# Fixed places in the engines' order for the transposes, the rounded stationary and gate times up of an expert block

## The chip, the cores and the metric

One core of a Trainium2 chip runs the whole program in one launch. The metric is the time of an execution on the device in microseconds; where several were measured, their median. The engines are named as in the profile: PE is TensorE's matmul row, PEld its weight loads, DVE is VectorE, ACT is ScalarE, POOL is GpSimd, SP is SyncE, which issues the weight transfers.

## What is computed

Two float32 model blocks, one behind the other, on 256 tokens of width 1024. The first has two layers of feed-forward, four mixers and feed-forward. The second has a pooling mixer with a feed-forward, and a delta-rule mixer with a mixture of experts. The change lies in the last of these alone:

```python
N_EXPERTS, TOP_K, EXPERT_FF = 8, 2, 3584
logits = (t @ router_w) + router_b
top_vals, top_idx = lax.top_k(logits, TOP_K)
gates = jnp.sum(one_hot(top_idx, N_EXPERTS) * softmax(top_vals)[..., None], axis=1)
for e in range(N_EXPERTS):
    y = (silu(t @ w_gate[e]) * (t @ w_up[e])) @ w_down[e]
    out = out + gates[:, e:e + 1] * y
```

## The kernel before, in words

The first 1.6 ms hold the other layers and don't change. In the expert stage (function `short`) the eight experts are taken in the order of their token counts. For each, the tokens that chose it are gathered into the columns of a stationary tile `XG`. An expert's 3584 inner columns are done in seven blocks of 512, so there are 56 steps. Each step streams 12 weight tiles of 128x1024 float32 (512 KB each) from HBM into a ring of 23 buffers `raw` (8 + 11 + 4): four for the gate product, four for the up product, four for the down product.

Products are made in a rounded float32 format. So each weight tile is split in `halves` (lines 328 to 338): ScalarE writes the rounded tile `hi` (line 336), VectorE writes the rest `lo = raw - hi` (line 337), and only then can `raw` be loaded again. There are five `hi` and four `lo` buffers. Tokens are split likewise. Experts of which `FEW` is true (six of eight) have at most 64 tokens: their rounded tokens and the rests lie side by side in one 128-column stationary, so a `hi` or `lo` tile is multiplied once, and the two halves of the result are added by a matmul with a constant matrix `BOTH`. The last of the eight tiles of gate and up is used unsplit, as full float32 against `XF` (two matmul rows for each 512 columns). So a few-token step has 11 `hi` and 11 `lo`. The two other experts split tokens in two stationaries and make three products for each tile, 12 `hi` and 12 `lo`.

One step's way: `gate_up` (line 1931) fills two PSUM banks `gu`; `finish` (line 1957) makes `sl`, first Silu of the gate bank on ScalarE (line 1959), then gate times up, times the row scale, on VectorE (line 1960). `down` (line 1964) turns `sl` by four TensorE transposes into the PSUM tile `x`, splits that into the stationary `hh` (`split`, lines 362 and 363: the rounded part on ScalarE, the rest on VectorE, in the same tile for few-token experts, in `hl` for the others), splits four weight tiles and multiplies them into two PSUM banks `y`. After the seventh block `scatter` adds `y` to the result `ACC`.

The steps are laid over each other: the loop at the end of `short` calls `gate_up` of a block first, then `down` of the block before; the new block's `finish` is called inside that `down`. A scheduler then sets each engine's order by its own estimates of time; each engine runs its list strictly in that order, so an instruction that waits holds all behind it. The helper `queued` (line 1917) adds an order without a wait: its instruction may not stand earlier on its engine than the one named. Before, two things are tied so: the copy of the gate bank for `BOTH` (line 1929), and the Silu, behind the `hi` of the down product's first tile.

Of the kernel before, what the change touches and what calls it, by code (L numbers as in the profile page):

```python
# [9 lines left out]
F32 = mybir.dt.float32  # L10
F32R = mybir.dt.float32r
I32 = mybir.dt.int32
BF16 = mybir.dt.bfloat16
AF = mybir.ActivationFunctionType
OP = mybir.AluOpType
# [3 lines left out]
P = 128  # L19
# [4 lines left out]
NE = 8  # L24
# [37 lines left out]
FEW = [r not in (1, 2) for r in PLACES]  # L62
# [186 lines left out]
class _K:  # L249
# [78 lines left out]
    def halves(self, raw, parts=1):  # L328

        nc = self.nc  # L330
        self.npart += 1
        hi, lo = [self.T(ps[self.npart % len(ps)], [P, 1024], n, F32R) for ps, n in ((self.his, "hi"), (self.los, "lo"))]
        n = 1024 // parts
        for i in range(parts):
            c = slice(i * n, i * n + n)
            self.last_hi = nc.scalar.activation(hi[:, c], raw[:, c], AF.Copy)  # L336
            nc.vector.tensor_tensor(lo[:, c], raw[:, c], hi[:, c].bitcast(F32), OP.subtract)  # L337
        return hi, lo

    def chunk(self, ap):  # L340
# [1501 lines left out]
    def short(self, HH, HL, ACC, RS, keyp, keyl, GTp, BOTH, where, st):  # L1842
# [3 lines left out]
        nc, tc = self.nc, self.tc  # L1846

        def open_(name, bufs):
            return st.enter_context(tc.tile_pool(name=name, bufs=bufs))

        pool, p1 = open_("few", 2), open_("few1", 1)
# [65 lines left out]
        def queued(ins, first):  # L1917

            if first is not None:
                self.tc.add_manual_dep(  # L1920
                    ins.ins, first.ins.name,
                    mybir.DependencyInfo(mybir.DependencyClass.NoSync, mybir.DependencyReason.DATA),
                    reason="order on an engine")

        both = []

        def copy_gate(ps):
            both.append(self.T(p1, [P, 512], "both"))
            queued(nc.scalar.activation(both[-1], ps, AF.Copy), self.last_hi)

        def gate_up(e, fb, XG, RX, XF):
            gu = []
            for m in range(2):
                ps = self.T(self.psg, [P, 512], "gu")
                for q in range(2):
                    raws = [self.load_half(where(e)[fb * 6 + m * 2 + q], j) for j in range(2)]
                    whole = m and q and FEW[e]
                    ch = [self.halves(r) for r in raws[0:1 if whole else 2]]
                    if m and not q and FEW[e]:
                        copy_gate(gu[0])  # L1940
                    for kk in range(4):
                        k = q * 4 + kk
                        c = slice((kk % 2) * 512, (kk % 2) * 512 + 512)
                        if whole and kk > 1:
                            self.mm(ps, ps, XF[:, kk - 2, :], raws[1][:, c], False, k == DT - 1)
                            continue
                        wh, wl = ch[kk // 2]
                        self.mm(ps, ps, XG[:, 0, k, :], wh[:, c], k == 0, False)
                        if not FEW[e]:
                            self.mm(ps, ps, XG[:, 1, k, :], wh[:, c], False, False)  # L1950
                        self.mm(ps, ps, XG[:, 0, k, :], wl[:, c], False, k == DT - 1)
                gu.append(ps)
            if FEW[e]:
                self.mm(gu[0], gu[0], BOTH, both[-1], True, True)
            sl = self.T(pool, [P, 512], "sl")

            def finish(hi):

                queued(nc.scalar.activation(sl, gu[0], AF.Silu, scale=RX), hi)
                nc.vector.scalar_tensor_tensor(sl, gu[1], RX, sl, OP.mult, OP.mult)  # L1960

            return sl, finish

        def down(e, fb, sl, ya, OT, fin=None):
            ps = self.T(self.psx, [P, 512], "x")
            p4 = ps.rearrange("p (a b) -> p a b", a=4)
            hh = self.T(pool, [P, 4, P], "hh", F32R)
            if FEW[e]:
                n = slice(0, 64)
                for i in range(4):  # L1970
                    self.mm(ps, p4[:, i, n], sl[:, i * P:i * P + P], BOTH[:, n], True, True)
                self.split(p4[:, :, n], hh[:, :, n], hh[:, :, 64:])
            else:
                for i in range(4):
                    self.tr(p4[:, i, :], sl[:, i * P:i * P + P])
                hl = self.T(p1, [P, 4, P], "hl", F32R)
                self.split(p4, hh, hl)
            end = (e, fb) == (NE - 1, 6)
            if end:
                raws = [self.load_half(where(e)[fb * 6 + 4 + j // 2], j % 2, 2) for j in range(4)]  # L1980
                self.gb, self.fin = self.raw(), self.raw()
                nc.sync.dma_start(self.gb, self.A["prow"][:, 24:24 + D].partition_broadcast(P))
            for n in range(2):
                if not end:
                    raws = [self.load_half(where(e)[fb * 6 + 4 + n], j) for j in range(2)]
                    ch = [self.halves(raws[0])]
                    if n == 0 and fin:
                        fin(self.last_hi)
                    ch.append(self.halves(raws[1]))
                for i in range(4):  # L1990
                    c = slice((i % 2) * 512, (i % 2) * 512 + 512)
                    first, last = fb == 0 and i == 0, fb == 6 and i == 3
                    if end and i % 2 == 0:
                        w = self.halves(raws[2 * n + i // 2], 2)
                    wh, wl = w if end else ch[i // 2]
                    self.mm(ya[n], ya[n], hh[:, i, :], wh[:, c], first, False)
                    if not FEW[e]:
                        self.mm(ya[n], ya[n], hl[:, i, :], wh[:, c], False, False)
                    self.mm(ya[n], ya[n], hh[:, i, :], wl[:, c], False, last)
            if fb == 6:  # L2000
                for n in range(2):
                    scatter(e, n, ya[n], OT, end)

        def scatter(e, n, y, OT, end):
            yh = self.T(late[0], [P, 512], f"yh{n}", F32R)
            yl = self.T(late[0], [P, 512], f"yl{n}", F32R)
            self.split(y, yh, yl)
            c = slice(n * 512, n * 512 + 512)
            for t in range(2):
                ps = self.T(self.psx, [P, 512], "x")  # L2010
                self.mm(ps, ps, OT[:, t, :], yh, True, False)
                self.mm(ps, ps, OT[:, t, :], yl, False, True)
                nc.vector.scalar_tensor_tensor(ACC[:, t, c], ps, GTp[:, t, e:e + 1], ACC[:, t, c], OP.mult, OP.add)
                if end:
                    self.squares(ACC, t, n)

        steps = [(e, fb) for e in range(NE) for fb in range(7)]
        G = []
        for _ in gather([0]):
            pass  # L2020
        ya, pend = None, None
        for e, fb in steps + [(None, None)]:
            if e is not None:
                if (e, fb) == (0, 5):
                    self.early.close()
                    early.close()
                    px.append(open_("fewx2", 1))
                    late.append(open_("fewy", 1))
                sl, fin = gate_up(e, fb, G[e][0], *G[e][2:4])
            if pend is None:  # L2030
                fin(None)
            else:
                pe, pf, psl, pg = pend
                if pf == 0:
                    ya = [self.T(self.psy, [P, 512], f"y{n}") for n in range(2)]
                down(pe, pf, psl, ya, pg, fin if e is not None else None)
                es = [1] if pe == 0 else [pe + 1, pe + 2] if pe % 2 and pe < NE - 1 else None
                if pf == 4 and es:
                    for _ in gather(es):
                        pass  # L2040
            pend = (e, fb, sl, G[e][1]) if e is not None else None

    def moe(self, HH, HL, ACC, RS, GT, key, ci, few):
        nc, tc = self.nc, self.tc
# [148 lines left out]
```

## Time and profile before

| | |
|---|---|
| time, median of 3 runs | 2562.23 us (2560.03 to 2562.67) |
| the profiled execution | 2560.89 us, of which the span 2559.0 us |
| instructions | 45163 |
| expert stage, from the first gate matmul | 1629.2 us to the end of the span |
| mean granted TensorE clock | 0.994 |

The span runs from the first to the last instruction; the rest of an execution's time lies around it. The views used below: the page's busy shares; stretches of the span, chosen here to begin and end at a Silu (`sl` on ScalarE), which happens once in a step; the list of who waited for whom; and the timeline of one engine, in which like instructions next to each other are merged into one row, with the idle time ahead of the row and what ended it in brackets.

### The profile page before, as it was taken

The page shows a single profiled execution, that of the slowest core. Times are in us where ns is not written, and L with a number is a line of the kernel's source. Part 1 is how long each engine was busy: PE and PEld are TensorE (multiplying, and loading weights), DVE is VectorE, ACT ScalarE, POOL GpSimd, SP SyncE. Part 2 cuts the span into 40 slices and gives each one's busy share as a digit, 9 for nine tenths or more (in the row PEclk, how much of TensorE's full clock was granted, in tenths as well). Part 3 has the DMA queues.
Part 4 walks back from the last instruction along what each step waited for, and adds up shares of the span by engine and source line. Part 5 has one row for each costly group of instructions (what it writes and reads, how often), then busy time and mean ns, then how long its engine had stood idle before and what let it go on. Part 6 is the DMA issues. An engine that isn't in the chain of part 4 may idle for free. (4 is left out here: it accounts for less than half of the span.)

```text
span 2559.0 us, 45163 instructions
## 1 busy us (share of the span) xinstructions
PE 2501.5 (98%) x16795; PEld 2200.1 (86%) x16795; DVE 1933.5 (76%) x2621; ACT 1554.7 (61%) x2218; POOL 94.9 (4%) x99
## 2 busy tenths in 40 slices
PE   8999999999999999999999999899999999999997
PEld 8999899999999799999999998777766876677764
DVE  7657566666666667666765786799988898889887
ACT  5445464444445365445544675788777777777776
POOL 0003000000002100000000010000000000000000
PEclk9999999999999999999999999899999999999999
DMA  7655124555665233555566434899999999999994
GB/s 237 191 182 164 66 91 131 184 185 184 185 188 166 83 97 113 189 184 184 169 187 188 144 122 167 310 404 409 408 392 377 360 342 402 388 384 356 366 381 169
DMA packets 166915, 603.13 MB, mean 236 GB/s; under 512 B 18736, under 2 KB 19264, under 8 KB 166688
## 3 DMA queue, kind: packets, MB, share of 16 engines
q1 hardware_dynamic: 165792, 596.92, 66.5%
q0 software_dynamic: 896, 3.27, 0.4%
q8 instruction: 133, 2.18, 0.4%
q14 instruction: 94, 0.77, 0.1%
HBM read 596.96 MB, written 2.10 MB: 234 GB/s over the span
## 5 line engine op out<-in xcount | busy, mean ns | idle before, releaser
L337 DVE TENSOR_TENSOR lo<-raw,hi 128x1024 fp32r<-128x1024 f32 x1086 | 1290.2, 1221 | 337.7 <-ACT hi L336 329.9
L336 ACT ACTIVATE hi<-raw 128x1024 fp32r<-128x1024 f32 x1086 | 1104.2, 1052 | 621.9 <-issue 324.8
L264 PE MATMUL m<-xh,hi 128*128 128x256 f32 x1760 | 495.7, 282 | 8.5 <-ACT xh L365 7.9
L264 PE MATMUL m<-xh,lo 128*128 128x256 f32 x1760 | 495.8, 282 | 2.6 <-DVE lo L337 2.5
L264 PE MATMUL m<-xl,hi 128*128 128x256 f32 x1760 | 495.3, 282 | 1.8 <-DVE xl L366 1.8
L264 PE MATMUL gu<-hi,XG 128*128 128x512 f32 x1036 | 373.4, 399 | 0.2
L264 PE MATMUL gu<-lo,XG 128*128 128x512 f32 x812 | 347.5, 430 | 5.9 <-DVE lo L337 5.3
L264 PEld LDWEIGHTS m<-xh,hi 128*128 128x128 f32 x1760 | 333.5, 189 | 9.2 <-ACT xh L365 8.3
L264 PEld LDWEIGHTS m<-xh,lo 128*128 128x128 f32 x1760 | 333.2, 189 | 3.5 <-DVE lo L337 3.5
L264 PEld LDWEIGHTS m<-xl,hi 128*128 128x128 f32 x1760 | 333.1, 189 | 2.4 <-DVE xl L366 2.4
L264 PE MATMUL mm<-hl,hi 128*128 128x256 f32 x880 | 248.2, 282 | 0.0
L264 PE MATMUL mm<-hh,lo 128*128 128x256 f32 x880 | 248.2, 282 | 0.0
L264 PE MATMUL mm<-hh,hi 128*128 128x256 f32 x880 | 247.6, 282 | 0.0
L264 PE MATMUL mm<-xh,hi 128*128 128x256 f32 x832 | 240.6, 290 | 6.0 <-DVE x L1133 3.1
L264 PE MATMUL mm<-xl,hi 128*128 128x256 f32 x832 | 239.3, 288 | 0.0
L264 PEld LDWEIGHTS gu<-hi,XG 128*128 128x128 f32 x1036 | 195.4, 189 | 50.2 <-ACT hi L336 7.8
L264 PE MATMUL mm<-xh,lo 128*128 128x256 f32 x832 | 237.9, 286 | 0.1
L264 PEld LDWEIGHTS gu<-lo,XG 128*128 128x128 f32 x812 | 153.1, 189 | 94.4 <-DVE lo L337 59.9
L264 PE MATMUL y<-hi,hh 128*128 128x512 f32 x448 | 193.4, 435 | 0.0
L264 PE MATMUL y<-lo,hh 128*128 128x512 f32 x448 | 181.3, 410 | 6.5 <-DVE lo L337 6.3
L264 PEld LDWEIGHTS mm<-hl,hi 128*128 128x128 f32 x880 | 168.2, 191 | 0.0
L264 PEld LDWEIGHTS mm<-hh,lo 128*128 128x128 f32 x880 | 168.2, 191 | 0.0
(589 smaller groups left out, 3501.6 us busy)
## 6 DMA issues: line engine op xcount, KB each, us to landing
raw<-in_moe SPq DMA_DIRECT2D x668, 512.0 KB, 6.4
raw<-in_ffn SPq DMA_DIRECT2D x330, 512.0 KB, 3.5
raw<-in_win SPq DMA_DIRECT2D x56, 512.0 KB, 3.5
raw<-in_dnin SPq DMA_DIRECT2D x32, 512.0 KB, 3.8
raw<-in_wout SPq DMA_DIRECT2D x16, 512.0 KB, 3.5
raw<-in_pin SPq DMA_DIRECT2D x8, 512.0 KB, 3.6
raw<-in_dnout SPq DMA_DIRECT2D x8, 512.0 KB, 3.6
raw<-in_moe SPq DMA_DIRECT2D x8, 256.0 KB, 6.2
```

What stands on the lines that cost most here:

```text
L264: ins = self.nc.tensor.matmul(out, lhsT=lhsT, rhs=rhs, start=start, stop=stop)
L336: self.last_hi = nc.scalar.activation(hi[:, c], raw[:, c], AF.Copy)
L337: nc.vector.tensor_tensor(lo[:, c], raw[:, c], hi[:, c].bitcast(F32), OP.subtract)
```

## The change

`halves` keeps the `lo` instruction as it kept the `hi`. In `gate_up` the first `hi` and `lo` of the gate product's second half are remembered (its third tile). `finish` becomes a function of its own with a place for each of its two instructions: the Silu stays behind the `hi` of the down product's first tile; gate times up is now tied behind the `lo` of the down product's last tile. In `down` the first transpose is tied behind the last `y` matmul of the block before; the rounded part and the rest of `hh` are tied behind the remembered `hi` and `lo` of the next block's gate product, save in the very last block. The helper `split` is written out for this. No instruction is added or removed.

```diff
@@ halves
-            nc.vector.tensor_tensor(lo[:, c], raw[:, c], hi[:, c].bitcast(F32), OP.subtract)
+            self.last_lo = nc.vector.tensor_tensor(lo[:, c], raw[:, c], hi[:, c].bitcast(F32), OP.subtract)
@@ short, gate_up
-        both = []
+        both, mark = [], {}
...
-                    ch = [self.halves(r) for r in raws[0:1 if whole else 2]]
+                    ch = [self.halves(raws[0])]
+                    if m == 0 and q == 1:
+                        mark.update(hi=self.last_hi, lo=self.last_lo)
+                    if not whole:
+                        ch.append(self.halves(raws[1]))
...
-            def finish(hi):
-
+            return sl, gu, RX
+
+        def finish(sl, gu, RX, hi, lo):
+
+            if hi is not None or lo is None:
                 queued(nc.scalar.activation(sl, gu[0], AF.Silu, scale=RX), hi)
-                nc.vector.scalar_tensor_tensor(sl, gu[1], RX, sl, OP.mult, OP.mult)
-
-            return sl, finish
+            if lo is not None or hi is None:
+                queued(nc.vector.scalar_tensor_tensor(sl, gu[1], RX, sl, OP.mult, OP.mult), lo)
@@ short, down
+            end = (e, fb) == (NE - 1, 6)
+
+            for i in range(4):
+                if FEW[e]:
+                    ins = self.mm(ps, p4[:, i, 0:64], sl[:, i * P:i * P + P], BOTH[:, 0:64], True, True)
+                else:
+                    ins = nc.tensor.transpose(p4[:, i, :], sl[:, i * P:i * P + P], self.c("ident"))
+                if i == 0:
+                    queued(ins, mark.get("y"))
+            src, parts = p4, [hh, None]
             if FEW[e]:
-                n = slice(0, 64)
-                for i in range(4):
-                    self.mm(ps, p4[:, i, n], sl[:, i * P:i * P + P], BOTH[:, n], True, True)
-                self.split(p4[:, :, n], hh[:, :, n], hh[:, :, 64:])
+                src, parts = p4[:, :, 0:64], [hh[:, :, 0:64], hh[:, :, 64:]]
             else:
-                for i in range(4):
-                    self.tr(p4[:, i, :], sl[:, i * P:i * P + P])
-                hl = self.T(p1, [P, 4, P], "hl", F32R)
-                self.split(p4, hh, hl)
-            end = (e, fb) == (NE - 1, 6)
+                hl = parts[1] = self.T(p1, [P, 4, P], "hl", F32R)
+            queued(nc.scalar.activation(parts[0], src, AF.Copy), None if end else mark["hi"])
+            queued(nc.vector.tensor_tensor(parts[1], src, parts[0].bitcast(F32), OP.subtract), None if end else mark["lo"])
...
                     ch = [self.halves(raws[0])]
                     if n == 0 and fin:
-                        fin(self.last_hi)
+                        finish(*fin, self.last_hi, None)
                     ch.append(self.halves(raws[1]))
+                    if n == 1 and fin:
+                        finish(*fin, None, self.last_lo)
...
-                    self.mm(ya[n], ya[n], hh[:, i, :], wl[:, c], False, last)
+                    mark["y"] = self.mm(ya[n], ya[n], hh[:, i, :], wl[:, c], False, last)
```

What the scheduler makes of it, in the fifth and sixth block of the third expert (few tokens; the numbers behind a name tell tiles apart, and some of the changed kernel are lower by one than the same tile's before). First VectorE, from the `lo` of the down product's first tile on, before:

```order
L337 TENSOR_TENSOR lo_22480<-raw_22475,hi_22479 128x1024
L1960 SCALAR_TENSOR_TENSOR sl_22466<-gu_22428,RX_21705,sl_22466 128x512
L337 TENSOR_TENSOR lo_22486<-raw_22477,hi_22485 128x1024
L337 TENSOR_TENSOR lo_22502<-raw_22497,hi_22501 128x1024
L363 TENSOR_TENSOR hh_22598<-x_22597,hh_22598 128x4x64
L337 TENSOR_TENSOR lo_22506<-raw_22499,hi_22505 128x1024
L337 TENSOR_TENSOR lo_22523<-raw_22518,hi_22522 128x1024
```

and of the change:

```order
L337 TENSOR_TENSOR lo_22480<-raw_22475,hi_22479 128x1024
L337 TENSOR_TENSOR lo_22485<-raw_22477,hi_22484 128x1024
L337 TENSOR_TENSOR lo_22501<-raw_22496,hi_22500 128x1024
L337 TENSOR_TENSOR lo_22505<-raw_22498,hi_22504 128x1024
L1968 SCALAR_TENSOR_TENSOR sl_22466<-gu_22428,RX_21705,sl_22466 128x512
L337 TENSOR_TENSOR lo_22523<-raw_22518,hi_22522 128x1024
L337 TENSOR_TENSOR lo_22527<-raw_22520,hi_22526 128x1024
L337 TENSOR_TENSOR lo_22543<-raw_22538,hi_22542 128x1024
L1989 TENSOR_TENSOR hh_22598<-x_22597,hh_22598 128x4x64
L337 TENSOR_TENSOR lo_22547<-raw_22540,hi_22546 128x1024
```

The four `lo` of the down product now stand together, `sl` behind them, and the rest of `hh` behind the third `lo` of the next gate product, not between the third and fourth of the down product. In the first expert and the beginning of the second `sl` stands behind the four `lo` in both kernels.

TensorE, at the same place (`x` are the transposes of `sl`, four of them in the one row), before:

```order
L264 MATMUL y_4041_22075<-lo_22480,hh_22468 128x512
L264 MATMUL y_4041_22075<-hi_22485,hh_22468 128x512
L264 MATMUL x_22597<-BOTH_19686,sl_22466 128x64 x4
L264 MATMUL y_4042_22076<-hi_22501,hh_22468 128x512
L264 MATMUL y_4041_22075<-lo_22486,hh_22468 128x512
```

and of the change:

```order
L264 MATMUL y_4042_22076<-hi_22504,hh_22468 128x512
L264 MATMUL y_4042_22076<-lo_22505,hh_22468 128x512
L264 MATMUL gu_22517<-hi_22522,XG_3910_21609 128x512
L264 MATMUL x_22597<-BOTH_19686,sl_22466 128x64 x4
L264 MATMUL gu_22517<-lo_22523,XG_3910_21609 128x512
```

The transposes stood behind the fifth of the sixteen `y` matmuls; now they stand behind the sixteenth and the first gate matmul of the next block.

ScalarE, one block earlier (fourth to fifth), before:

```order
L1959 ACTIVATE sl_22336<-gu_22257,RX_21705 128x512
L336 ACTIVATE hi_22355<-raw_22347 128x1024
L336 ACTIVATE hi_22371<-raw_22367 128x1024
L362 ACTIVATE hh_22468<-x_22467 128x4x64
L336 ACTIVATE hi_22375<-raw_22369 128x1024
L336 ACTIVATE hi_22392<-raw_22388 128x1024
```

and of the change:

```order
L1966 ACTIVATE sl_22336<-gu_22257,RX_21705 128x512
L336 ACTIVATE hi_22354<-raw_22347 128x1024
L336 ACTIVATE hi_22370<-raw_22366 128x1024
L336 ACTIVATE hi_22374<-raw_22368 128x1024
L336 ACTIVATE hi_22392<-raw_22388 128x1024
L336 ACTIVATE hi_22396<-raw_22390 128x1024
L336 ACTIVATE hi_22412<-raw_22408 128x1024
L1988 ACTIVATE hh_22468<-x_22467 128x4x64
L336 ACTIVATE hi_22416<-raw_22410 128x1024
```

`hh` moves from behind the third of the down product's four `hi` to behind the third `hi` of the next gate product. SP's list of transfers is the same in both kernels.

## Rows read from the trace of the kernel before

**Rows 1.** The page: busy us, share of the span, instructions by engine.
```profile
PE 2501.5 (98%) x16795; PEld 2200.1 (86%) x16795; DVE 1933.5 (76%) x2621; ACT 1554.7 (61%) x2218; POOL 94.9 (4%) x99
```

**Rows 2.** Stretches of the expert stage, us; busy time by engine.
```profile
core 0: us, PE busy (x) PEld busy (x) DVE busy (x) ACT busy (x) POOL busy (x), PEclk, DMA share, GB/s
1662.30:1690.10 27.80, 27.80 (x117) 20.32 (x116) 27.43 (x27) 24.67 (x29) 0.00 (x0) 1.00 1.01 398
1843.20:1876.60 33.40, 31.85 (x125) 21.13 (x125) 31.11 (x33) 25.12 (x31) 0.00 (x0) 1.00 0.99 376
1876.60:1939.70 63.10, 61.69 (x234) 38.36 (x233) 54.81 (x53) 47.87 (x57) 0.00 (x0) 1.00 1.03 409
1939.70:1976.20 36.50, 35.30 (x147) 25.67 (x146) 32.48 (x34) 26.45 (x31) 0.21 (x1) 1.00 0.98 365
2009.00:2026.20 17.20, 17.20 (x78) 13.82 (x77) 15.00 (x15) 13.09 (x16) 0.00 (x0) 1.00 0.99 364
2116.30:2195.20 78.90, 77.14 (x292) 47.94 (x291) 68.53 (x66) 59.85 (x71) 0.20 (x1) 1.00 1.03 402
2228.70:2260.20 31.50, 30.80 (x118) 19.13 (x117) 27.35 (x27) 23.89 (x29) 0.00 (x0) 1.00 1.03 409
2260.20:2331.30 71.10, 69.85 (x323) 52.99 (x322) 62.07 (x69) 54.03 (x77) 0.46 (x1) 1.00 0.97 367
2434.10:2467.60 33.50, 33.10 (x134) 22.86 (x133) 31.23 (x33) 25.22 (x32) 0.00 (x0) 1.00 0.98 361
2467.60:2530.70 63.10, 61.70 (x234) 38.36 (x233) 54.82 (x53) 47.90 (x58) 0.00 (x0) 1.00 0.84 331
```

**Rows 3.** Who waited for whom, 1600 to 2550 us: total in us, times, longest.
```profile
ACT hh L362 <- PE x L264: 70.6, 33, 2.8
...
DVE sl L1960 <- PE gu L264: 60.3, 39, 2.3
PEld gu L264 <- DVE lo L337: 59.9, 156, 1.0
...
PEld y L264 <- DVE lo L337: 20.7, 36, 1.1
```

**Rows 4.** Timeline, DVE, late step: start, duration, instruction, [idle before].
```profile
1895.64 0.75 DVE L1960 SCALAR_TENSOR_TENSOR sl<-gu,RX,sl 128x512 f32<-128x512 f32 x1 [1.70 <-PE gu L264]
...
1898.58 0.42 DVE L363 TENSOR_TENSOR hh<-x,hh 128x256 fp32r<-128x256 f32 x1
1898.95 8.04 DVE L337 TENSOR_TENSOR lo<-raw,hi 128x1024 fp32r<-128x1024 f32 x7
```

**Rows 5.** Timeline of DVE in an early step.
```profile
1678.86 0.75 DVE L1960 SCALAR_TENSOR_TENSOR sl<-gu,RX,sl 128x512 f32<-128x512 f32 x1 [0.38 <-PE gu L264]
1679.54 4.63 DVE L337 TENSOR_TENSOR lo<-raw,hi 128x1024 fp32r<-128x1024 f32 x4
```

**Rows 6.** Instruction groups, 1629 to 2551 us: busy, mean ns | idle before.
```profile
L337 DVE TENSOR_TENSOR lo<-raw,hi 128x1024 fp32r<-128x1024 f32 x622 | 723.4, 1219 | 22.2 <-ACT hi L336 15.2 <-PE gu L264 3.0 <-issue 2.5
L336 ACT ACTIVATE hi<-raw 128x1024 fp32r<-128x1024 f32 x621 | 616.3, 1052 | 32.5 <-PE gu L264 15.3 <-PE y L264 12.8 <-DMA raw<-in_moe 1.3
```

**Rows 7.** Timeline of PE in an early step.
```profile
1682.10 1.00 PE L264 MATMUL x<-BOTH,sl 128*128 128x64 f32 x8
1682.91 0.48 PE L264 MATMUL gu<-lo,XG 128*128 128x512 f32 x1
...
1685.80 0.39 PE L264 MATMUL gu<-hi,XG 128*128 128x512 f32 x1
```

**Rows 8.** Timeline of ACT in a late step.
```profile
1897.59 0.39 ACT L362 ACTIVATE hh<-x 128x256 fp32r<-128x256 f32 x1 [2.63 <-PE x L264]
1897.87 2.00 ACT L336 ACTIVATE hi<-raw 128x1024 fp32r<-128x1024 f32 x2
```

**Rows 9.** SP waits; transfers, median us to landing; 1600 to 2550 us.
```profile
SPq L325 <- DVE lo L337: 395.3, 475, 6.6
...
raw<-in_moe SPq DMA_DIRECT2D x647, 512.0 KB, 6.3
```

More of the change, by code (lines that the diff above doesn't have):

```diff
@@ L2028, in short @@
                     late.append(open_("fewy", 1))
-                sl, fin = gate_up(e, fb, G[e][0], *G[e][2:4])
+                fin = gate_up(e, fb, G[e][0], *G[e][2:4])
             if pend is None:
-                fin(None)
+                finish(*fin, None, None)
             else:
@@ L2040, in short @@
                         pass
-            pend = (e, fb, sl, G[e][1]) if e is not None else None
+            pend = (e, fb, fin[0], G[e][1]) if e is not None else None
     def moe(self, HH, HL, ACC, RS, GT, key, ci, few):
```

## The prediction

> **What bounds the kernel now.** I read the page first: TensorE 98% busy, VectorE 76% [rows 1]. That says only that TensorE is fed nearly everywhere; a matmul that waits for its operand is drawn longer, so the page's share can't show a small recurring wait. So I cut the expert stage into stretches [rows 2] and looked at what repeats. One block of a few-token expert (a "step" below, from one Silu to the next) takes two very different lengths. Early, two steps last 27.80 us, **13.90 each**. From the third expert on, four steps last 63.1 us, **15.78 each**; so do the stretches of five (78.9), two (31.5) and four (63.1): 15 steps, 236.6 us. The work is the same: VectorE is busy 27.43/2 = 13.7 us per step early and 54.81/4 = 13.7 us late. The late step holds 2.1 us in which VectorE does nothing; early TensorE has no idle time at all (27.80 of 27.80). The granted clock is 1.00, the 2.4 GHz level, in every one of these stretches, so no term is needed for it.
>
> By the matmul row alone, TensorE is idle 63.1 - 61.69 = 1.4 us of the four late steps, 0.35 us a step; filled, that would give 15 x 0.35 = 5 us. The Trainium skill (Perfetto Trace Analysis, Identifying the Most-Contended Engine) says that matmul busy share is a poor measure of what is left on that engine, and that the busy share of the weight loads tells it better; this trace bears it out, 61% late (38.36 of 63.1) against 73% early (20.32 of 27.80). An estimate by that page would be 15.78 x 61/73 = 13.2 us a step, 39 us over 15. I go by neither: the 13.90 us of the early rows is a duration that the chip has shown for this step.
>
> The waits name the loop [rows 3]: VectorE's `sl` waits for TensorE (`gu`, 60.3 us in 39 waits), the weight loads of TensorE wait for VectorE's `lo` (59.9 and 20.7), and ScalarE's `hh` waits for the transposes `x` (70.6). In time [rows 4]: late, `sl` is queued after the first of the four `lo` of the down product, gets there 1.70 us before the up product ends, and holds VectorE; the `lo` behind it then come late, and TensorE, which has by then finished the up product and needs exactly these, waits in turn. Each waits once a step for the other. Early, `sl` stands after all four `lo` and waits 0.38 us [rows 5].
>
> **The change, part by part, for one late step.**
> - `sl` on VectorE is tied behind the last `lo` of the down product (the order rows of VectorE). It moves three `lo` later, and three `lo` follow at 1.14 us each (8.04 us for seven, of which the last alone is drawn with its full 1.22 [rows 4, 6]), so it comes 3.4 us later against a wait of 1.70: the wait goes to nothing. Queued behind it are the next block's gate `lo`; they lose nothing, since the three `lo` that passed `sl` are ones TensorE needs first.
> - The four transposes go behind the last `y` matmul of the block before. In the early steps they take 0.81 us there, from the first to the next matmul [rows 7]; `sl` is then done while TensorE still has matmuls of the last `lo` to do, so no new wait: the early steps have the transposes at just this place and TensorE doesn't idle.
> - `hh` on ScalarE is tied behind the third gate `hi` of the next block, the rounding rest on VectorE behind the third `lo`. Late, ScalarE sat 2.63 us at `hh` [rows 8] with the down product's `hi` behind it. It will still sit there, since three gate `hi` are ready before `x` is, but with three more `hi` in store. This is the tight place: the fourth `hi` and `lo` of the gate are behind it. From the end of `x`: 0.03 to `hh`, 0.28 to the next `hi` [rows 8], 1.05 for it, 1.22 for its `lo` [rows 6], and some 0.08 for two handovers: 2.7. TensorE meanwhile has 12 matmuls from 1682.91 to 1685.80 [rows 7]; the end of `x` is 0.19 after the first of these, so 2.89 - 0.19 = 2.7. Even; the early steps put `hh` one or two `hi` later and so show no loss here. I give it 0.1 us a step; its bounds are 0 and 0.7 (the 0.39 of `hh` and two more handovers counted twice).
> - Nothing is added or taken away: no matmul, no transfer, no conversion. The order of the transfers on SP's queue is the same; only the moment at which buffers come free shifts.
>
> So a late step becomes 13.90 + 0.1 = **14.0 us**: 15 x (15.78 - 14.0) = **26.6 us**.
> - The four first-and-second steps of an expert with the scatter of the one before (33.4, 33.5 us; the first and the last are in rows 2) hold one such wait each, but VectorE is busy for 31.1 of the 33.4 us, so at most 2.3 can go. I take the wait alone, 1.7: 4 x 1.7 = **6.8 us** (bounds 0 and 9.2).
> - 1939.7 to 1976.2 (few-token to many-token expert, VectorE busy 32.48 of 36.50): one wait, **1.7 us** (0 to 2.7). 2260.2 to 2331.3 (TensorE busy 69.85 of 71.10): **2.5 us** (0 to 5). A gather lies in it; around gathers the order of conversions and gather matmuls shifts too, with the same instructions, which I cost at 0 within 2 us, since TensorE has work there throughout.
> - Steps of many-token experts (14; 17.20 us, TensorE busy 17.20 [rows 2]): TensorE bound, VectorE has 2.2 us to spare: 0. Here 16 three-product matmuls stand between `x` and the fourth `lo`, more than the 2.7 us of the chain: 0.
> - The first expert's steps are in the wanted order already: 0. The tail: transposes behind the last `y` leave TensorE without work for about the 0.39 + 0.42 us of the two halves of `hh` [rows 8, 4], and the tail's own `sl` wait (another 1.7) goes: 0 within 1.
>
> Sum: 26.6 + 6.8 + 1.7 + 2.5 = 37.6 us. The profiled execution took 2560.89 us (span 2559.0, 1.9 around it), 1.3 below the median of 2562.23. 2560.9 - 37.6 = 2523.3; I say **2523**.
>
> **What the transfers allow.** A faster step asks for weights faster. A step reads 12 loads of 0.524 MB = 6.29 MB; at the 409 GB/s of the late stretch [rows 2] these take 15.4 us, more than 14.0. But the loads run ahead: SP waits for `lo` to free a buffer (395.3 us in 475 waits), ScalarE for a load only 1.3 us in all [rows 9, 6]. The ring has 8 + 11 + 4 = 23 buffers; a load takes 6.3 us from issue to landing, which at 1.28 us each is 5 under way, so some 16 are landed and unread. A 14.0 us step uses 12 and gets 10.9: 1.1 lost a step. The longest run between two slow steps that refill, experts four and five, has 7 fast steps and two pairs that about hold level: 8 of the 16. The cover lasts. The early 13.90 us steps ran at 398 GB/s on such a lead.
>
> **The rivals.**
> - *Half of it*: the chain through `hh` turns out at its upper bound, 0.7 us or more a step, and the pairs give nothing: 15 x (15.78 - 14.6) = 18, with the small terms 20: 2541. For it: `hh` is one or two `hi` earlier than in the early steps. Against: the sum above comes out even.
> - *The transfers take over*: the lead doesn't cover it and a step falls to the 15.4 us of its loads: 15 x 0.4 = 6, and 3 of the other terms: 2552. For it: 409 GB/s is the most that any stretch shows, with the DMA share at 1.03. Against: the landed lead and the early steps. The Trainium skill (DMA: Bandwidth & Descriptors, Where 436 GB/s comes from) puts the HBM side at about 358 GB/s for a core; by that the step couldn't go below 17.6 us, slower than it is, and the trace disagrees with 409 GB/s for 63 us on end.
> - *Slower*: three fixed places make one chain out of what the scheduler had kept apart: last `lo`, `sl`, `x`, `hh`, next `hi`, next `lo`. Where VectorE isn't ahead when the down product starts, TensorE comes to the transposes before `sl` is done and stands for it. Price: `sl` 0.75 and the rest's 0.42 and 0.39 of `hh`, together 1.5 us on each of the 42 few-token steps, 63 us, less the 37.6: 2586. It decides from 0.9 us a step (37.6/42). For it: the many gather and scatter steps, where VectorE is late. Against: the early steps, with the same places for `sl` and `x`, show no wait of TensorE for `sl`.
>
> **How the numbers follow.** My case 0.76; half of it 0.13; transfers 0.06; slower 0.05. My case alone spans 2512 (upper bounds: 15 x 1.88 = 28, 9, 2.7, 5 and a few us of transitions) to 2535. The range reaches on into the half case: **2509 to 2544**. A measurement of this kernel tells apart about 0.2%, 5 us. Faster by more: my case, the half, and half of the transfer case, 0.92; the other half and a slow case near its tie, 0.04; slower 0.04.
>
> **What would show it.** In the changed profile the total of `sl` waiting for `gu` should fall from 60.3 to under 10 us, the weight loads' waits for `lo` from 81 to under 25, and stretches of few-token steps should repeat every 14.0 us with a weight-load share above 70%. `hh` waiting for `x` may stay. ScalarE's `hi` waiting for loads beyond a few us would show that the transfers bind. TensorE waiting for `sl` at `x`, or steps of 15 us and more with a new wait of the gate's fourth `lo` for `hi`, would show me wrong.

## The result, and the profile after

The changed kernel takes **2525.34 us** (median; 2524.44 to 2527.58) against 2562.45 for the kernel before in the same comparison: a ratio of 0.9858, 95% interval 0.9841 to 0.9875. The prediction was 2523, range 2509 to 2544. The profiled execution after has a span of 2523.4 us, 35.6 less than before.

The page's busy shares hardly move, though 36 us are gone; only the weight loads show it, 88% for 86% [rows 1].

```profile
PE 2474.6 (98%) x16795; PEld 2210.8 (88%) x16795; DVE 1933.9 (77%) x2621; ACT 1557.6 (62%) x2218; POOL 95.6 (4%) x99
```

The stretches of [rows 2], cut at the same Silus; 1965.20 to 1982.10, the first step after an expert change, is new:

```profile
core 0: us, PE busy (x) PEld busy (x) DVE busy (x) ACT busy (x) POOL busy (x), PEclk, DMA share, GB/s
1663.00:1690.80 27.80, 27.80 (x117) 20.33 (x116) 27.43 (x28) 24.67 (x29) 0.00 (x0) 1.00 1.01 391
1844.40:1876.10 31.70, 31.35 (x125) 21.28 (x125) 31.01 (x33) 25.20 (x31) 0.00 (x0) 1.00 1.01 387
1876.10:1932.70 56.60, 56.60 (x234) 40.33 (x233) 54.69 (x53) 47.95 (x58) 0.00 (x0) 1.00 1.03 409
1932.70:1965.20 32.50, 32.46 (x143) 25.37 (x141) 31.37 (x33) 26.29 (x31) 0.21 (x1) 1.00 1.03 409
1965.20:1982.10 16.90, 16.81 (x74) 13.66 (x75) 16.90 (x18) 13.23 (x15) 0.00 (x0) 1.00 1.03 408
1999.40:2016.50 17.10, 17.10 (x78) 13.87 (x77) 15.16 (x15) 13.05 (x15) 0.00 (x0) 1.00 1.03 409
2105.30:2175.90 70.60, 70.60 (x292) 50.25 (x291) 68.23 (x66) 59.82 (x71) 0.21 (x1) 1.00 1.03 409
2207.70:2235.90 28.20, 28.20 (x118) 20.10 (x117) 27.26 (x27) 23.89 (x29) 0.00 (x0) 1.00 1.03 409
2235.90:2303.00 67.10, 67.08 (x319) 52.76 (x317) 61.27 (x68) 54.30 (x77) 1.37 (x1) 1.00 1.03 408
2405.60:2438.30 32.70, 32.56 (x134) 23.02 (x133) 31.16 (x33) 25.39 (x31) 0.00 (x0) 1.00 0.97 355
2438.30:2494.90 56.60, 56.60 (x234) 40.34 (x233) 54.70 (x53) 47.98 (x58) 0.00 (x0) 1.00 0.94 369
```

Four late steps take 56.6 us instead of 63.1, five 70.6 instead of 78.9, two 28.2 instead of 31.5, the last four 56.6 instead of 63.1: **14.14 us** a step, and TensorE has no idle time in them. The early steps stay. The stretch with the first expert change, 36.5 us before, takes 32.5.

The waits, 1600 to 2515 us, and below them the group of `sl` on VectorE (busy, mean ns of one, idle time ahead of it):

```profile
ACT hh L1988 <- PE x L264: 48.0, 32, 2.4
...
PEld gu L264 <- DVE lo L337: 29.4, 87, 0.6
...
PEld y L264 <- DVE lo L337: 5.3, 22, 0.2
```
```profile
L1968 DVE SCALAR_TENSOR_TENSOR sl<-gu,RX,sl 128x512 f32<-128x512 f32 x56 | 41.8, 746 | 2.1 <-ACT sl L1966 1.3 <-PE gu L264 0.8
```

`sl` waited 60.3 us for `gu` before [rows 3]; 0.8 is left. The weight loads' waits for `lo` fall from 59.9 and 20.7 to 29.4 and 5.3. `hh` still waits for `x`, 48.0 after 70.6. The same late step, VectorE and then ScalarE; compare [rows 4, 8]:

```profile
1895.34 0.74 DVE L1968 SCALAR_TENSOR_TENSOR sl<-gu,RX,sl 128x512 f32<-128x512 f32 x1
1896.00 3.48 DVE L337 TENSOR_TENSOR lo<-raw,hi 128x1024 fp32r<-128x1024 f32 x3
1899.40 0.42 DVE L1989 TENSOR_TENSOR hh<-x,hh 128x256 fp32r<-128x256 f32 x1
1899.74 3.49 DVE L337 TENSOR_TENSOR lo<-raw,hi 128x1024 fp32r<-128x1024 f32 x3
1903.59 4.83 DVE L337 TENSOR_TENSOR lo<-raw,hi 128x1024 fp32r<-128x1024 f32 x4 [0.37 <-ACT hi L336]
```
```profile
1898.24 0.39 ACT L1988 ACTIVATE hh<-x 128x256 fp32r<-128x256 f32 x1 [1.61 <-PE x L264]
1898.52 2.94 ACT L336 ACTIVATE hi<-raw 128x1024 fp32r<-128x1024 f32 x3
```

`sl` starts with no wait. ScalarE still stands 1.61 us at `hh`. What is left of the tight place shows on TensorE, where a `gu<-lo` starts 0.36 and 0.32 us after the matmul ahead of it; 0.23 is usual:

```profile
1900.65 0.40 PE L264 MATMUL gu<-hi,XG 128*128 128x512 f32 x1
1901.01 0.51 PE L264 MATMUL gu<-lo,XG 128*128 128x512 f32 x1
...
1901.82 0.39 PE L264 MATMUL gu<-hi,XG 128*128 128x512 f32 x1
1902.14 0.50 PE L264 MATMUL gu<-lo,XG 128*128 128x512 f32 x1
```

These are the fourth and the fifth `lo` of the gate and up products, counted together; the fourth is done at 1899.74 + 1.22 [rows 6] = 1900.96.

SP's waits and transfers, against [rows 9]. SP waits less for `lo` to free a buffer, and more for transfers (247.4 us, 49.3 before). A transfer takes 9.8 us from issue to landing instead of 6.3; at 1.28 us each (0.524 MB at 409 GB/s) I estimate 7.7 under way at a time instead of 5.

```profile
SPq L325 <- DVE lo L337: 230.8, 298, 6.5
```
```profile
raw<-in_moe SPq DMA_DIRECT2D x648, 512.0 KB, 9.8
```

### The profile page after: what moved, and what is told of

The parts are those of the page before. It is cut to its first block, busy times and chain, and to the rows that moved or that the text cites. A ratio compares the mean times of both kernels' runs of the same rounds, so it can differ in the third digit from the quotient of the medians.

```text
span 2523.4 us, 45260 instructions
## 1 busy us (share of the span) xinstructions
PE 2474.6 (98%) x16795; PEld 2210.8 (88%) x16795; DVE 1933.9 (77%) x2621; ACT 1557.6 (62%) x2218; POOL 95.6 (4%) x99
## 5 line engine op out<-in xcount | busy, mean ns | idle before, releaser
L264 PEld LDWEIGHTS gu<-lo,XG 128*128 128x128 f32 x812 | 153.2, 189 | 66.6 <-DVE lo L337 29.4
```

The source lines that it names most:

```text
L264: ins = self.nc.tensor.matmul(out, lhsT=lhsT, rhs=rhs, start=start, stop=stop)
```

## The experiments

Each is an edit of the changed kernel. "Step" is the mean, from Silu to Silu in the profile, of the first four late few-token steps in a row (in the third expert).

| run | median us (range) | ratio to before, 95% | step us |
|---|---|---|---|
| the change | 2525.34 (2524.44 to 2527.58) | 0.9858 [0.9841, 0.9875] | 14.14 |
| tie of `sl` alone | 2544.35 (2542.57 to 2546.88) | 0.9923 [0.9908, 0.9938] | 15.15 |
| all ties but `sl` | 2568.53 (2563.12 to 2572.05) | 1.0017 [1.0008, 1.0026] | 15.73 |
| `sl` behind the second `lo` | 2537.55 (2534.3 to 2540.13) | 0.9905 [0.9888, 0.9921] | 14.52 |
| `sl` behind the third `lo` | 2531.32 (2526.37 to 2535.55) | 0.9883 [0.9866, 0.9899] | 14.13 |
| `hh` one tile later | 2524.87 (2523.81 to 2525.53) | 0.9848 [0.9834, 0.9861] | 14.03 |
| `hh` two tiles later | 2521.93 (2519.22 to 2523.88) | 0.9834 [0.9821, 0.9847] | 13.93 |
| rest of `hh` alone one later | 2531.19 (2528.41 to 2534.43) | 0.9882 [0.9865, 0.99] | 14.35 |
| rest of `hh` alone two later | 2521.1 (2520.14 to 2522.89) | 0.9841 [0.9825, 0.9857] | 14.03 |
| no tie of the transposes | 2528.63 (2524.64 to 2533.64) | 0.9881 [0.9865, 0.9896] | 14.13 |
| ring of 14 | 2532.16 (2531.42 to 2534.48) | 0.9891 [0.9876, 0.9906] | 14.13, later to 15.36 |
| `hh` two later, tail reordered | 2519.66 (2518.95 to 2523.89) | 0.9845 [0.9831, 0.9858] | 13.93 |
| the change again | 2527.0 (2524.52 to 2528.06) | 0.9864 [0.9849, 0.9879] | 14.13 |

### Which tie brings the gain

The tie of `sl` alone:

```diff
-                    queued(ins, mark.get("y"))
+                    queued(ins, None)
...
-            queued(nc.scalar.activation(parts[0], src, AF.Copy), None if end else mark["hi"])
-            queued(nc.vector.tensor_tensor(parts[1], src, parts[0].bitcast(F32), OP.subtract), None if end else mark["lo"])
+            nc.scalar.activation(parts[0], src, AF.Copy)
+            nc.vector.tensor_tensor(parts[1], src, parts[0].bitcast(F32), OP.subtract)
```

> Only the tie of gate times up is kept; the transposes and both halves of hh go back to the scheduler. In the steady few-token block sl and the transposes then stand where they do in the changed kernel, but hh stands one gate tile earlier (behind the second hi and lo of the next gate product). If the wait of sl was the whole cause, and hh may stand anywhere: late step 14.1 us, total 2525 as the changed kernel, within 3. If the place of hh sets the chain from the transposes to the next hi and lo, as my prediction has it: 8 matmuls of 0.24 us cover the chain instead of 12, so each late step is 0.9 to 1.0 longer than the changed kernel's 14.13, 15.1 us; over the 15 late steps 14 us, with the first expert's and the pairs' steps up to twice that: 2539 to 2550.

And all ties but that of `sl`, which is created after the first `lo` of the down product and left to the scheduler:

```diff
-                queued(nc.vector.scalar_tensor_tensor(sl, gu[1], RX, sl, OP.mult, OP.mult), lo)
+                queued(nc.vector.scalar_tensor_tensor(sl, gu[1], RX, sl, OP.mult, OP.mult), lo or None)
...
-                        finish(*fin, self.last_hi, None)
+                        finish(*fin, self.last_hi, False)
...
-                    if n == 1 and fin:
-                        finish(*fin, None, self.last_lo)
```

> The transposes and hh stay tied as in the change, gate times up alone is left to the scheduler, which puts it behind the first lo of the down product again, as before. If the mutual wait of sl and the lo behind it is the cause of the late step: sl waits 1.5 us or more for gu in each late step again (total of 55 us and more), the late step is 15.5 to 16 us, total 2555 to 2570. If instead the new places of the transposes or of hh bring the gain: sl may wait, but steps stay near 14.1 to 14.5, total 2525 to 2532.

Without the tie of `sl` nothing is gained (2568.5, 0.2% slower than before): `sl` is back behind the first `lo` and stands there. The list of waits and the timeline of VectorE in that run:

```profile
DVE sl L1968 <- PE gu L264: 66.7, 41, 2.6
```
```profile
1899.27 0.75 DVE L1968 SCALAR_TENSOR_TENSOR sl<-gu,RX,sl 128x512 f32<-128x512 f32 x1 [1.71 <-PE gu L264]
```

With that tie alone half the gain comes. The step is 15.15 us, 1.01 over the changed kernel's, as the place of `hh` one tile (four matmuls) earlier should cost. In that run, a stretch of four steps with TensorE idle for 3.0 us, ScalarE at `hh`, and VectorE, whose third gate `lo` now waits for ScalarE's `hi` behind `hh`:

```profile
1877.40:1938.00 60.60, 57.58 (x234) 39.98 (x233) 55.35 (x53) 47.86 (x57) 0.00 (x0) 1.00 1.03 409
```
```profile
1900.59 0.38 ACT L1988 ACTIVATE hh<-x 128x256 fp32r<-128x256 f32 x1 [2.56 <-PE x L264]
```
```profile
1901.95 4.63 DVE L337 TENSOR_TENSOR lo<-raw,hi 128x1024 fp32r<-128x1024 f32 x4 [0.52 <-ACT hi L336]
```

So the tie of `sl` is what the gain rests on, and it gives half alone; the later place of `hh` gives the other half, and only with `sl` out of the way.

The third tie, of the transposes:

```diff
-                    queued(ins, mark.get("y"))
+                    queued(ins, None)
```

> The transposes are left to the scheduler; gate times up and hh stay tied as in the change. The order in the steady few-token block comes out as in the changed kernel (transposes behind the last y and the first gate matmul), so this tie should be worth nothing there: late step 14.1 us, total 2525 within 3. If the tie of the transposes carries a part of the gain by the order at other places (scatters, gathers, the tail): over 2529.

Steps of 14.13 us, and the profiled execution took 2524.64; but the median of four is 2528.63 with a spread of 9 us. In the steady block the tie is worth nothing, as expected; whether it is worth a few us elsewhere, the spread leaves open. In the one execution with a trace the stage lasts 854.0 us from its first Silu to its last, in the change 853.3; single steps of the second and third expert differ by up to 4.5 us, both ways.

### How much of the wait costs how much

`sl` behind the second `lo`, and behind the third:

```diff
-                    if n == 1 and fin:
+                    if n == 0 and fin:
                         finish(*fin, None, self.last_lo)
```
```diff
-                    ch.append(self.halves(raws[1]))
                     if n == 1 and fin:
                         finish(*fin, None, self.last_lo)
+                    ch.append(self.halves(raws[1]))
```

> The change, but gate times up tied behind the second lo of the down product instead of the fourth. It gets there one lo (1.14 us) later than behind the first, so 0.56 of the wait of 1.70 should be left. If each microsecond that VectorE stands at sl lengthens the step: 14.13 + 0.5 to 0.6 = 14.7 us, sl waiting about 0.5 us a step, total 2533 to 2540. If any lo queued behind sl costs, waiting or not (TensorE needs it first): 15 us and more, total over 2540. If a half microsecond disappears in VectorE's own slack: 14.1 to 14.3, total 2525 to 2529.

> The same behind the third lo: sl gets there after the up product's end by the before trace (2.28 later against a wait of 1.70). If the wait is all: no wait, late step 14.13, total 2525 within 3. If any lo queued behind sl costs its 0.66 us: 14.5 to 14.8, total 2532 to 2540.

VectorE in a late step of the two runs:

```profile
1893.98 0.75 DVE L1968 SCALAR_TENSOR_TENSOR sl<-gu,RX,sl 128x512 f32<-128x512 f32 x1 [0.30 <-PE gu L264]
```
```profile
1893.84 0.74 DVE L1968 SCALAR_TENSOR_TENSOR sl<-gu,RX,sl 128x512 f32<-128x512 f32 x1
```

Behind the second `lo` 0.30 us of wait is left (0.5 was expected) and the step is 14.52, some 0.4 over the change. With the run without the tie (1.71 us of wait, 15.73, 1.6 over) that is roughly a microsecond of step for a microsecond of wait. Behind the third `lo` there is no wait and the step is 14.13: it is the wait that costs, not the place. The median of that run, 2531.32, lies over the expected 2525 to 2528, though its profiled execution took 2526.37; its four times spread over 9 us, and only one of them has a trace. That one lasts 854.4 us from the first Silu to the last, 1.1 more than the change.

### Where the last 0.24 us of the step are

`hh` behind the fourth gate tile, then behind the fifth:

```diff
-                    if m == 0 and q == 1:
-                        mark.update(hi=self.last_hi, lo=self.last_lo)
                     if not whole:
                         ch.append(self.halves(raws[1]))
+                    if m == 0 and q == 1:
+                        mark.update(hi=self.last_hi, lo=self.last_lo)
```
```diff
-                    if m == 0 and q == 1:
+                    if m == 1 and q == 0:
                         mark.update(hi=self.last_hi, lo=self.last_lo)
```

> hh tied one gate tile later than in the change (behind the fourth hi and lo instead of the third), all else as in the change: 16 matmuls cover the chain from the transposes to the next hi and lo instead of 12. If the 0.24 us that a late step lasts over 13.90 is this chain's overflow: late step 13.9, the delay at the fourth gate lo gone, 15 x 0.24 = 3.6 us and up to 2 more in the pairs: 2520 to 2522. If the 0.24 comes from somewhere else (transfers, the stand of the weight loads): 2525 within 2, with steps of 14.13.

> hh tied two gate tiles later than in the change (behind the first hi and lo of the up product). Chain theory: as with one tile later, late step 13.9, total 2520 to 2522, nothing more, since 16 matmuls already cover it. If a later hh delays the down product (its stationary is needed only after the up product, some 3 us later): steps above 14.1 and a wait of the weight loads of y for hh, total above 2525.

One tile later brought half of what was expected, two tiles all of it. So I split the two halves of `hh`: ScalarE's stays behind the third `hi`, VectorE's goes behind the fourth `lo` or behind the fifth:

```diff
-                        mark.update(hi=self.last_hi, lo=self.last_lo)
+                        mark["hi"] = self.last_hi
...
                         ch.append(self.halves(raws[1]))
+                    if m == 0 and q == 1:
+                        mark["lo"] = self.last_lo
```
```diff
-                        mark.update(hi=self.last_hi, lo=self.last_lo)
+                        mark["hi"] = self.last_hi
+                    if m == 1 and q == 0:
+                        mark["lo"] = self.last_lo
```

> Only VectorE's half of hh moves: the rest is tied behind the fourth gate lo, while ScalarE's rounded half stays behind the third gate hi as in the change. Two readings of the 0.24 us that the late step lasts over 13.90. ScalarE theory (my prediction's chain from the transposes over hh to the fourth hi): nothing changes, step 14.13, total 2525 within 3. VectorE theory (it has no idle time from sl to the fifth gate lo, and its half of hh, 0.34 us, stands ahead of the fourth lo that TensorE waits for): the fourth lo is in time, the fifth is late instead as with both halves moved, step 14.0 to 14.06, total 2522 to 2525.

> The same with VectorE's half behind the fifth lo (the first of the up product). ScalarE theory: step 14.13, total 2525 within 3. VectorE theory: as with both halves moved that far, step 13.90 to 13.96, total 2520 to 2523.

Neither theory alone holds. VectorE's half two tiles later gives 14.03 us: 0.11 less than the change, 0.10 more than with both halves moved. So at the change's place VectorE's half costs 0.11, and ScalarE's half, with VectorE's out of the way, another 0.10. ScalarE's was not moved alone, so the two shares are known in this order only. TensorE bears the split out: with VectorE's half two tiles later the matmul of the fourth `lo` starts 0.23 us after the one ahead (0.36 in the change), that of the fifth still 0.32. One tile later is worse than either end, 14.35. VectorE in that run:

```profile
1900.17 1.23 DVE L337 TENSOR_TENSOR lo<-raw,hi 128x1024 fp32r<-128x1024 f32 x1 [0.26 <-ACT hi L336]
1901.32 0.42 DVE L1991 TENSOR_TENSOR hh<-x,hh 128x256 fp32r<-128x256 f32 x1
1901.65 4.75 DVE L337 TENSOR_TENSOR lo<-raw,hi 128x1024 fp32r<-128x1024 f32 x4
```

The fourth `lo` waits 0.26 us for the `hi` that ScalarE made late, and then `hh` stands before the fifth. On TensorE the matmul of the fourth then starts in time, 0.24 us after the one ahead, and that of the fifth 0.65 us after it. In the change `hh` lies in that gap, where most of its 0.34 us would have been idle time.

### Whether the transfers have cover

```diff
-NRB, NRC, NRD, NRE, NRF = 8, 11, 3, 0, 1
+NRB, NRC, NRD, NRE, NRF = 8, 2, 3, 0, 1
```

> The changed kernel with a ring of 14 weight buffers instead of 23, the order in the steady block as in the change. If the lead of landed buffers is what lets a step of 14.1 us run at loads of 15.4 us (6.29 MB at 409 GB/s): with nine buffers fewer the lead of some 16 is 7 at most and is used up within a run of few-token steps; the later ones then last 15.0 to 15.5 us, ScalarE's hi waits for loads there, total 2530 to 2545. If the loads are no limit at all at this pace: steps of 14.1 throughout, total 2525 within 3.

The long run of fast steps that the prediction names, in that kernel: the third and fourth of the five, the fifth, and then the two of the next expert. Below it ScalarE in the last one.

```profile
2136.50:2164.70 28.20, 28.20 (x117) 20.07 (x117) 27.25 (x27) 23.90 (x29) 0.00 (x0) 1.00 1.03 409
2164.70:2179.60 14.90, 14.90 (x63) 10.63 (x62) 14.10 (x14) 12.34 (x15) 0.20 (x1) 1.00 1.03 409
...
2211.00:2225.90 14.90, 14.90 (x63) 10.62 (x62) 14.11 (x14) 12.41 (x16) 0.00 (x0) 1.00 1.03 408
2225.90:2241.20 15.30, 15.03 (x62) 10.16 (x61) 13.83 (x13) 12.74 (x15) 0.00 (x0) 1.00 1.03 410
```
```profile
2231.34 1.06 ACT L336 ACTIVATE hi<-raw 128x1024 fp32r<-128x1024 f32 x1 [0.24 <-DMA raw<-in_moe]
2232.62 1.06 ACT L336 ACTIVATE hi<-raw 128x1024 fp32r<-128x1024 f32 x1 [0.21 <-DMA raw<-in_moe]
```

Four steps run at 14.13 us on the lead, the fifth takes 14.9, the first of the next two 14.82 (Silu to Silu), and the last, of which 15.30 lie in the stretch (15.36 from Silu to Silu), goes at the pace of the loads: ScalarE takes a tile every 1.28 us, as 0.524 MB at 409 GB/s come. In the other runs of late steps the short ring costs nothing. These three steps make 2.7 of the 5.6 us by which the span is longer than the change's; another 1.7 lie in the first two experts, 1.4 ahead of the stage. With 23 buffers no step shows this: the cover lasts, though of the 23 fewer than nine are to spare.

### The tail, and a better version

`hh` behind the fifth tile, and for the last block alone `sl` behind the second `lo` of the down product and the transposes behind the `y` matmuls of the first bank:

```diff
-            end = (e, fb) == (NE - 1, 6)
+            end, pre = (e, fb) == (NE - 1, 6), (e, fb) == (NE - 1, 5)
...
-                    if n == 1 and fin:
+                    if n == (0 if pre else 1) and fin:
...
-                    mark["y"] = self.mm(ya[n], ya[n], hh[:, i, :], wl[:, c], False, last)
+                    ins = self.mm(ya[n], ya[n], hh[:, i, :], wl[:, c], False, last)
+                    if not (pre and n):
+                        mark["y"] = ins
```

> hh tied behind the first hi and lo of the up product, as in the run before, and in the last block alone gate times up tied behind the second lo of the down product and the transposes behind the last y of the first bank, so that seven y matmuls of 0.23 us stand behind them. Expected if TensorE's 1.5 us at the last transposes is open time and what slowed the last y matmuls: 1.5 us less and no slow stretch behind it, another 1.5, against the run with hh at the same place (2521.9): 2518 to 2520.5. If the last y wait for their lo anyway: 2521 to 2523.

> The changed kernel itself, timed beside the three others: 2525 within 2, late steps 14.13 us. If it came out at 2522 or less, hh behind the fifth tile would be no gain over it.

TensorE in the tail with `hh` two tiles later, without this edit; the granted clock in the stretches is the third number from the end:

```profile
2499.19 0.50 PE L264 MATMUL y<-hi,hh 128*128 128x512 f32 x1 [1.50 <-DVE hh L1989]
```
```profile
2498.00:2500.00 2.00, 0.81 (x4) 0.68 (x5) 2.00 (x5) 1.67 (x4) 0.00 (x0) 1.00 0.00 0
2500.00:2502.00 2.00, 2.00 (x7) 1.62 (x6) 0.94 (x2) 0.03 (x1) 0.00 (x0) 0.61 0.00 0
2502.00:2504.00 2.00, 2.00 (x6) 1.52 (x6) 0.69 (x1) 0.57 (x1) 0.00 (x0) 0.53 0.00 0
```

and with it:

```profile
2498.00:2500.00 2.00, 1.97 (x9) 1.54 (x9) 2.00 (x5) 1.98 (x4) 0.00 (x0) 1.00 0.00 0
2500.00:2502.00 2.00, 2.00 (x10) 1.50 (x9) 2.00 (x4) 0.60 (x1) 0.00 (x0) 1.00 0.00 0
```

The standstill of 1.50 us is gone, and in these two profiles the tail from the last Silu is 27.2 us for 30.0 (the change: 28.5). All five times of the run (to 2523.89) lie under all four of the change beside it (from 2524.52), 7 us apart by the medians; the intervals of their ratios overlap by 0.0009. It has the lowest median here, but it isn't told apart from `hh` two tiles later alone: by medians it is ahead (2519.66 against 2521.93), by the ratios to the kernel before behind (0.9845 against 0.9834). Of the 2.8 us between the two tails some 1.5 is the lower clock, by the distances of the `y` matmuls; the change's tail had full clock, and against that one the edit gives 1.3.

## Why the prediction was right, and where it was off

- **The loop.** As told: `sl` held VectorE, the `lo` behind it held TensorE. Taking the wait back by its tie alone brings the old time back; leaving 0.30 of it brings 0.4 of the step back.
- **The late step.** Predicted 14.0, measured 14.14; 15 steps gave 236.75 - 212.04 = 24.7 us of the 26.6. The term that was too small is the 0.1 for the tight place. I followed the chain over ScalarE alone, and that part measures 0.10 once VectorE's is gone. What I left out is VectorE's half of `hh`, which stands ahead of the fourth `lo` in its own queue: another 0.11. The remaining 0.03 is in the step even with both halves out of the way (13.93). The "half of it" rival, a chain of 0.7 and more, is the kernel with `hh` one tile earlier (1.0 over the change), not this one.
- **The four pairs.** 4.9 us of the 6.8. The two behind few-token experts gave 1.7 each as booked (33.4 to 31.75). The two behind many-token experts gave 0.74 each: their first step still holds three-product `y` matmuls of the many-token expert, and in the last of them TensorE is now busy 32.56 of 32.70 while VectorE has 1.5 to spare. I bounded the pairs by VectorE's busy time alone. The row of TensorE before (33.10 of 33.50, [rows 2]) points at it, but is no bound: 0.40 was idle there and 0.74 came.
- **The two transitions.** Booked 1.7 and 2.5; they gave 2.9 and 3.0. The stretches named fell by 4.0 each, the first by more than its upper bound of 2.7, since they held a further wait of `sl`, some 2 us, in the expert change that I had not counted; the first step of the many-token expert after each grew by 1.0. In the first of these VectorE now has no idle time (16.90 of 16.90) and TensorE 0.09.
- **Booked at nothing.** Many-token steps: 17.2 as before. In the run with `sl` behind the second `lo`, `sl` waits up to 1.5 us in them and they take 17.2 all the same. The last of the second many-token expert gave 1.3 that I had not booked. The first two experts cost 0.5 more, the part ahead of the expert stage 0.7 and the tail 0.2. In all 24.7 + 4.9 + 2.9 + 3.0 + 1.3 + 0.2 for small ones, less 1.4, is 35.6; 37.6 was predicted. That the sum is only 2.0 off is in part luck: shortfalls of 5.2 (1.9 in the loop, 1.9 in the pairs, 1.4 of extra cost) stand against 3.2 that I had not booked.
- **Transfers.** Their rival fell: 409 GB/s in the late stretches, no step at the 15.4 us of its loads, ScalarE's `hi` waiting 1.6 us for loads in all. With nine buffers fewer it comes true, at 15.4 us and in the expert named. The Trainium skill (DMA: Bandwidth & Descriptors, Where 436 GB/s comes from) puts the HBM side at about 358 GB/s for a core, as half of a stack's 716; this program runs on one core alone, and the trace after stays at 409 for 70.6 us on end.
- **Slower.** TensorE doesn't wait for `sl` at the transposes. In the last block it stands for `hh`, as foreseen, but 1.50 us and not 0.8; against the tail's own `sl` wait, which is gone, that came to the 0.2 above.
- **What should show.** `sl` waiting for `gu` 0.8 us (under 10 was said), weight-load share 40.33 / 56.60 = 71% (over 70), steps of 14.1 (14.0); the loads' waits for `lo` 34.7, not under 25. The two places above are little of that: with both halves of `hh` two tiles later 31.8 are left, and the step is 13.93 all the same. So these waits are no measure of lost time here. The Trainium skill (Perfetto Trace Analysis, Identifying the Most-Contended Engine) has the weight loads' share tell what is left: the estimate by it was 13.2 us a step. The best step seen here, 13.93, is at 40.66 / 55.70 = 73%, the share of the early steps, so as a sign it held; the time was better taken from a step that the chip had shown.

## What to carry to other kernels

Where two engines each wait for the other once a period and no engine is full, look for one instruction that is queued ahead of work which the engine that it waits for needs first; here the place was right when the wait was gone, and further was worth nothing (14.13 us behind the third `lo`, 14.14 behind the fourth). Before costing a place, run the chain through every queue that it passes, not only through the longest: here each half of one small split cost a tenth of a microsecond a step. Take what a stretch can give back from a like stretch that runs without the wait, and from the busy time of engines whose instructions keep their length, as VectorE's did. TensorE's busy row was no bound: four late steps with 1.4 us of it idle gave back 6.5.

## What the runs showed of the hardware that was not expected

TensorE's granted clock fell to 0.53 to 0.61, about the 1.2 GHz level, for some 3 us in one tail after TensorE had stood 1.50 us, with `y` matmuls 0.43 us apart instead of 0.23; the changed kernel stood as long at the same place in its profile and kept 1.00:

```profile
2503.00:2505.00 2.00, 0.89 (x4) 0.76 (x5) 2.00 (x5) 1.59 (x4) 0.00 (x0) 1.00 0.00 0
2505.00:2507.00 2.00, 2.00 (x10) 1.61 (x9) 0.95 (x3) 0.60 (x1) 0.00 (x0) 1.00 0.00 0
```

The change again, profiled, was 2.8 us longer than the first time, all of it before the first Silu of the expert stage (at 1644.48 us, the first time at 1641.62); from there to the end it took 881.7 us, the first time 881.8. The instructions are the same; in four of the 40 us slices the clock reads 0.96 where it read 1.00. One of them, the first time and again:

```profile
280.00:320.00 40.00, 40.00 (x294) 34.91 (x293) 23.66 (x39) 21.33 (x35) 3.96 (x3) 1.00 0.20 64
```
```profile
280.00:320.00 40.00, 40.00 (x285) 35.31 (x284) 23.30 (x38) 20.60 (x35) 3.96 (x3) 0.96 0.21 64
```

So nearly 3 us between two executions of one program lie in the first 1.6 ms here, and a single time tells no smaller difference. Over all thirteen profiles of the change and its variants the first Silu starts between 1640.0 and 1644.5 us. From there to the end `hh` two tiles later takes 878.4 us and the version with the tail reordered 874.2.
